# Row-tile loads and transposes in batches of three instead of one by one

## The chip, the cores and the metric

The kernel runs on one core of a Trainium2 chip. The metric is device time in microseconds, the median of several executions. A core has a matrix engine (PE, with its weight loads shown as PEld), a vector engine (DVE), a scalar engine (ACT), GpSimd (POOL) and SyncE (SP). Each works through its own list of instructions in order; semaphores tie the lists together. Here POOL and SP mostly issue DMAs.

## The reference

```python
def reference(x, w1, w2):          # x: 16 x 512 x 1024, w1 and w2: 1024 x 768, float32
    y1 = np.matmul(x, w1)
    y2 = np.matmul(x, w2)
    return (np.tanh(y1) * y2).astype(np.float32)
```

The rows of x are 16 x 512 = 8192, which makes 64 row tiles of 128 rows. Both products have the same left side.

## The kernel before, in words

**Tiles.** A row tile mt (0 to 63) goes through these steps. A load on POOL's queue (`load_x`, L353) brings it from device memory and casts it to fp16 into one of 8 buffers `xh`. A DMA transpose issued by SP (`transpose`, L378) turns it into one of 12 buffers `xT`, so that the contraction lies along the partitions. ACT sums its absolute values (`abs_x`, L381) for a range check at the end.

**Head and triples.** The first 4 tiles (HEAD) are multiplied plainly (`mm`, L421) while the weights come in. The other 60 form 20 triples (i = 0 to 19). Tile HEAD + 3i + r is row r of triple i. Tiles 0 to 6 are transposed by PE; from tile 7 on (BY_PE, so from triple 1) they are transposed by DMA, which makes 57 of them.

**A triple.** Its two halves of K times three row tiles against blocks of the two weights are computed by a scheme with fewer products: 15 products p0 to p14, each 4 matmuls with 512 columns (`product`, L444). Their left sides are either one half of a transposed tile or a sum or difference of such halves, made by DVE (`x_sum`, L412, ten per triple, named S3, S11, ... and written to a part of `early_x`). Their right sides are blocks of the weights `wh` or sums of blocks `b` (`w_sum`, L403). The products are combined in PSUM banks by ACT (`c_copy`, L448) and DVE (`c_add`, L454), then tanh on ACT (`c_tanh`, L457) and the multiplication on DVE (`c_mul`, L462) give the output tile `o`, which a store (L418) on SP's queue writes out. In each triple p7 is first and reads the third tile's transposed half directly; the first sums are S3 (first tile alone) and S11 (S3 with the second tile).

**Order.** PE's order of products is written out by hand (`PE_ORDER`). For the other engines a `Planner` simulates all operations with costs, due times and assumed DMA times, and emits them in the order of their planned starts. What it emits is then fixed for each engine. Its assumptions on when DMAs land (`lands`, `latency`, `LANDING`) thus change only the order, and an instruction that stands too early in an engine's list makes that engine wait.

**Holding the loads.** POOL would issue loads as early as buffers allow. A tiny copy on POOL from a transposed tile (`hold_loads`, L481) makes POOL wait until that transpose has landed:

```python
    def hold_loads(e, mt):
        pin(nc.gpsimd.tensor_copy(held, xt(mt)[:, 0, :1]))
```

Before the change, three loads (7, 8, 9) are free, and each later load mt waits for the transpose of tile max(mt - 4, 7). Transposes follow one another in tile order on SP, each after its own load; stores stand between them where the planner put them.

**Buffers.** A load into `xh` waits until the tile that was there before (8 tiles earlier) was transposed and summed by ACT. A transpose into `xT` waits for the last readers of the tile 12 before it, which is four triples.

Of the kernel before, what the change touches and what calls it, by code (L numbers as in the profile page):

```python
# [74 lines left out]
class Planner:  # L75
# [9 lines left out]
    def op(self, name, engines, due, needs, fn, *args, behind=(), issued=(), chains=(), xfer=0.0, latency=None, seeds=False,  # L85
           lands=None, hold=0.0):
        assert name not in self.ops, name
        self.ops[name] = dict(engines=engines, due=due, needs=[n for n in needs if n], behind=[n for n in behind if n], issued=[n for n in issued if n], fn=fn, args=args,
                              chains=chains, xfer=xfer, latency=latency, seeds=seeds, lands=lands, hold=hold)
        for c in chains:  # L90
            self.chains.setdefault(c, {"left": 0, "bank": None, "end": 0.0, "act": 0.0, "dve": 0.0})["left"] += 1
# [135 lines left out]
def kernel(  # L227
# [13 lines left out]
    MT = B * M // P  # L241
    F = 512
    G = N - F
    HEAD = 4
    TRIPLES = (MT - HEAD) // 3
    BY_PE = HEAD + 3
    FP32 = ((0, 0), (1, 0))
    LOW, HIGH = 512.0, 1024.0
    XT_BUFS, XH_BUFS, S_BUFS, O_BUFS, C_BUFS = 12, 8, 2, 9, 2
    WARM = 512, 512, 512, 512, 512, 512, 512  # L250
    FILL = 512, 512, 256
    AHEAD, FREE = 4, 3
    LANDING = {HEAD + 6: 5.8, HEAD + 7: 4.1, HEAD + 8: 3.9}
    S_AHEAD, HALVED = 4.0, 4
    LATER = {mt: 66.0 + 13.0 * mt for mt in range(HEAD - 1)}
    bf16, f16, f32, i32 = mybir.dt.bfloat16, mybir.dt.float16, mybir.dt.float32, mybir.dt.int32
# [39 lines left out]
    def xh_place(mt):  # L296
        return (mt - HEAD) % XH_BUFS

    def xh_before(mt):
        return next((m for m in range(mt - 1, 1, -1) if xh_place(m) == xh_place(mt)), None)  # L300
# [4 lines left out]
    op = plan.op  # L305
# [203 lines left out]
    rows_in = (HEAD + 2, HEAD, HEAD + 1)  # L509
# [3 lines left out]
    lands = dict(zip("x00 a0 x10 a1 x20 a2 x30 a3".split(), (4.31, 4.47, 6.13, 6.53, 7.7, 8.17, 9.05, 9.44)))  # L513
# [7 lines left out]
    for n, what in enumerate(on_sp):  # L521
        before = [f"L{on_sp[n - 1]}"] if n else []
        if what[0] == "x":
            op(f"L{what}", {"sp": 0.05}, 0.1 * n - 100, [], load_first, int(what[1]), int(what[2]), issued=before, lands=lands[what])
        else:
# [4 lines left out]
               behind=[f"c{a}{b}" for a, b in old], lands=lands[what])  # L530
# [3 lines left out]
    for n, mt in enumerate(rows_in):  # L534
        op(f"L{mt}", {"pool": 0.58}, 1 + 0.1 * n, [], load_x, mt, issued=[f"L{rows_in[n - 1]}" if n else f"c{late[-1]}"],
           behind=[f"cx{m}{h}" for m in range(2, HEAD) for h in range(2) if xh_place(m) == xh_place(mt)], lands=lands[f"x{mt}"])

    landed = {}
    for s, k in slices:
        loads = [f"g{k % KH}{t}" for t in range(2)] if s == "g" else [f"{s}{k}"]  # L540
# [30 lines left out]
    xt_readers = {mt: [] for mt in range(MT)}  # L571
# [12 lines left out]
    def reuse_out(mt):  # L584
        return [f"st{mt - O_BUFS}"] if mt >= HEAD + O_BUFS else []
# [16 lines left out]
    for n, s in enumerate("agb"):  # L602
        for mt in range(HEAD):
            if (s, mt) == ("b", HEAD - 1):
                continue
            due, behind = (lambda n: landed[slices["agb".index(s) * KO + n]] + 0.8 + 0.02 * mt), []
            finals(mt, s, due(KO - 1) + (5.0, 3.0, 7.0)["agb".index(s)], plain(mt, s, due, behind))

    mt = HEAD - 1
# [57 lines left out]
    for i in range(TRIPLES):  # L667
# [3 lines left out]
        for v, a, b, how in A_SUMS:  # L671
            op(f"S{v}.{i}", {"dve": 0.335}, None, x_needs(i, a) + x_needs(i, b), x_sum, i, v, a, b, how,
               hold=needed(i, v) - S_AHEAD if i > 1 else 0.0,
               behind=[f"{r}.{i - S_BUFS}" for r in a_readers[v]] if i >= S_BUFS else first_done)
# [3 lines left out]
        for o in C_OPS:  # L678
# [3 lines left out]
            if kind == "p":  # L682
                needs += x_needs(i, o[4]) + w_needs(o[5])
                op(f"{name}.{i}", {"pe": SLOT}, slot_of[i, name], needs, product, i, *o[3:], chains=chains,
                   behind=[f"m{HEAD - 1}y0{KO - 1}"] if (name, i) == ("p3", TRIPLES - 1) else [])
# [3 lines left out]
            if kind in ("seed", "copy", "add"):  # L689
                before = []  # L690
                if o[3][0] == "s":
                    before = [f"{r}.{i - C_BUFS}" for r in readers[o[3]]] if i >= C_BUFS else all_casts
# [5 lines left out]
            r = o[3]  # L698
            mt = HEAD + 3 * i + r
            due = soonest[i, name] + LAST  # L700
            if kind in ("t", "th"):
                lo, n = (0, F) if kind == "t" else (F, G)
                op(f"{name}.{i}", {"act": 0.5 if n == F else 0.285}, due, needs, c_tanh, i, r, o[4], lo, n, o[5],
                   behind=reuse_out(mt) + ([f"{FIRST_READER[name]}.{i}"] if i == TRIPLES - 1 and name in FIRST_READER else []), chains=chains)
# [4 lines left out]
            else:  # L709
                lo, n, at = (0, F, 0) if kind == "m" else (F, G, G)  # L710
                op(f"{name}.{i}", {"dve": 0.6 if n == F else 0.335}, due + 1, needs, c_mul, i, r, o[4], lo, n, at, chains=chains)
                outs[mt].insert(0 if kind == "m" else 1, f"{name}.{i}")
    for mt in range(MT):
# [14 lines left out]
                op(f"st{mt}{a}", {"sp": 0.4, "act": 0.4}, 2e4, part, store, mt, lo, n, xfer=0.4)  # L728
        else:
            op(f"st{mt}", {"sp": 0.05}, slot_of[max(i, 0), "p2"] + 12, outs[mt], store, mt, behind=late, xfer=1.0)  # L730
    for mt in range(BY_PE, MT):
        back = xh_before(mt)
        free = [] if back is None else ([f"PT{back}0", f"PT{back}1"] if back < BY_PE else [f"T{back}"]) + ([f"D{back}"] if back >= HEAD else [])
        before = f"L{mt - 1}" if mt > BY_PE else f"L{rows_in[-1]}"
        if mt >= BY_PE + FREE:
            op(f"H{mt}", {"pool": 0.1}, None, [f"T{max(mt - AHEAD, BY_PE)}"], hold_loads, max(mt - AHEAD, BY_PE), issued=[before])
            before = f"H{mt}"
        op(f"L{mt}", {"pool": 0.58}, None, [], load_x, mt, issued=[before], behind=free, xfer=XX)
        op(f"T{mt}", {"sp": 0.05}, None, [f"L{mt}"], transpose, mt, issued=[f"T{mt - 1}"] if mt > BY_PE else [],
           behind=xt_readers[mt - XT_BUFS] if mt >= XT_BUFS and mt - XT_BUFS != HEAD - 1 else [], xfer=1.2, latency=LANDING.get(mt, 1.0 if mt < HEAD + 6 else 3.0))  # L740
    for mt in range(HEAD, MT):
        i, r = divmod(mt - HEAD, 3)
        soon = START + 6 + 1.1 * r if i == 0 else slot_of[i, "p7"] + (2, 0, -4, -8)[min(i, 4) - 1] + 4.3 * r
# [125 lines left out]
```

## Time and profile before

| | |
|---|---|
| median of 3 runs | 297.87 us (297.68 to 299.07) |
| the profiled execution | 297.88 us |
| its span, first to last instruction | 296.3 us |
| granted clock of PE, mean | 0.997 |
| DVE busy | 257.4 us (87%) |
| ACT busy | 226.3 us (76%) |
| POOL busy | 49.2 us (17%) |
| DMA: loads of x by POOL | 60, of 256 KB in fp16, median 6.8 us from issue to landing |
| DMA: transposes by SP | 57, median 6.9 us |
| DMA: stores by SP, whole tiles | 58, of 384 KB, median 5.3 us |

The span lies inside the profiled execution's time; 1.6 us are around it. Times in the trace count from the start of the span. PE's busy time overlaps itself, since matmuls are pipelined and their ends are modelled, so rates are read from the starts.

### The profile page before, as it was taken

Reading aid. Unit: us, or ns where it says so; the run is one execution under the profiler, and the core shown is the slowest. Engines: PE = TensorE matmul, PEld = TensorE weight load, DVE = VectorE, ACT = ScalarE, POOL = GpSimd, SP = SyncE. Lnnn points to the kernel's source line nnn. Section 1 sums busy time; section 2 is a strip of 40 time slices with the busy share of each in tenths; the row PEclk is TensorE's granted clock in tenths of the full one; section 3 lists DMA queues with packets and bytes.
Section 4 is the critical chain, followed back from the end, with each engine's and each line's share of the span. In section 5 each row is a group of like instructions: output and inputs, shape, how many; then the busy total and the mean of one; then the engine's idle time right before and its main releaser. Section 6 shows DMA issues by size and latency. Waiting matters only on the chain. (4 is left out here: it accounts for less than half of the span.)

```text
span 296.3 us, 4677 instructions
## 1 busy us (share of the span) xinstructions
PE 289.6 (98%) x1374; PEld 131.9 (45%) x1374; DVE 257.4 (87%) x552; ACT 226.3 (76%) x453; POOL 49.2 (17%) x129
## 2 busy tenths in 40 slices
PE   7999999999999999999999999999999999999994
PEld 3344444444444444444444444444444444444442
DVE  1679899989999998888989898898989989898785
ACT  3586899699978979797797988768686776868442
POOL 0063033020213021102110120031012110000000
PEclk9999999999999999999999999999999999999998
DMA  6999999999999999999999999999999999340334
GB/s 215 388 307 204 183 160 149 229 197 237 224 253 271 215 198 252 237 144 253 233 234 162 221 191 218 195 310 223 221 235 232 261 269 298 127 162 25 136 141 164
DMA packets 84715, 63.51 MB, mean 214 GB/s; under 512 B 62800, under 2 KB 66896, under 8 KB 84688
## 3 DMA queue, kind: packets, MB, share of 16 engines
q1 hardware_dynamic: 73888, 44.84, 62.9%
q0 software_dynamic: 9792, 16.78, 37.2%
q10 hardware_dynamic: 1008, 1.57, 1.5%
q8 instruction: 11, 0.18, 0.3%
q14 instruction: 16, 0.13, 0.2%
HBM read 39.85 MB, written 25.17 MB: 219 GB/s over the span
## 5 line engine op out<-in xcount | busy, mean ns | idle before, releaser
L444 PE MATMUL bank<-b,early_x 128*128 128x512 f16 x640 | 148.3, 379 | 0.1
L444 PEld LDWEIGHTS <-early_x 128*128 128x128 f16 x800 | 78.1, 98 | 95.0 <-issue 0.7
L454 DVE TENSOR_TENSOR bank<-bank,arena 128x512 f32<-128x512 f32 x100 | 69.6, 697 | 14.4 <-ACT arena L448 8.8
L448 ACT ACTIVATE arena<-bank 128x512 f32<-128x512 f32 x100 | 59.4, 596 | 28.7 <-PE bank L444 28.5
L462 DVE TENSOR_TENSOR o<-o,bank 128x256 f32<-128x256 f32 (+1 forms) x132 | 64.3, 512 | 6.1 <-ACT o L457 5.4
L381 ACT ACTIVATE junk<-xh 128x1024 f16<-128x1024 f16 x60 | 63.3, 1054 | 0.2
L444 PEld LDWEIGHTS <-xT 128*128 128x128 f16 x400 | 39.0, 98 | 46.6 <-issue 0.3
L444 PE MATMUL bank<-b,xT 128*128 128x512 f16 x240 | 58.3, 379 | 0.0
L457 ACT ACTIVATE o<-bank 128x256 f32<-128x256 f32 (+1 forms) x80 | 34.5, 436 | 16.0 <-DVE bank L454 11.7
L444 PE MATMUL bank<-wh,xT 128*128 128x512 f16 x160 | 41.1, 379 | 0.0
L444 PE MATMUL bank<-wh,early_x 128*128 128x512 f16 x160 | 40.9, 379 | 0.0
L481 POOL CAST held<-xT 128x1 f32<-128x1 f16 x54 | 12.3, 227 | 159.4 <-DMA xT<-xh 159.3
L353 POOL DMA_DIRECT2D xh<-in_x_dram x60 | 31.9, 532 | 17.2 <-issue 7.7
L412 DVE TENSOR_TENSOR early_x<-early_x,xT 128x512 f16<-128x512 f16 x80 | 33.2, 419 | 0.5
L448 ACT ACTIVATE bank<-bank 128x512 f32<-128x512 f32 x40 | 21.5, 574 | 7.3 <-DVE bank L454 6.2
L457 ACT ACTIVATE o<-arena 128x512 f32<-128x512 f32 x40 | 25.1, 628 | 1.2 <-DVE arena L454 1.2
L421 PE MATMUL bank<-wh,xT 128*128 128x512 f16 x72 | 18.5, 379 | 0.5 <-DVE wh L359 0.3
L412 DVE TENSOR_TENSOR early_x<-xT,xT 128x512 f16<-128x512 f16 x40 | 16.8, 419 | 0.0
L412 DVE TENSOR_TENSOR early_x<-xT,early_x 128x512 f16<-128x512 f16 x40 | 16.8, 419 | 0.0
L454 DVE TENSOR_TENSOR bank<-arena,bank 128x512 f32<-128x512 f32 x20 | 13.9, 695 | 2.4 <-ACT o L457 0.9
L454 DVE TENSOR_TENSOR arena<-bank,arena 128x512 f32<-128x512 f32 x20 | 13.7, 683 | 0.2
L454 DVE TENSOR_TENSOR arena<-arena,bank 128x512 f32<-128x512 f32 x20 | 13.6, 681 | 0.0
(47 smaller groups left out, 134.7 us busy)
## 6 DMA issues: line engine op xcount, KB each, us to landing
out_dram<-o SPq DMA_DIRECT2D x58, 384.0 KB, 5.3
xh<-in_x_dram POOLq DMA_DIRECT2D x60, 256.0 KB, 6.8
arena<-in_w_dram SPq DMA_DIRECT2D x12, 256.0 KB, 5.6
early_x<-in_x_dram SPq DMA_DIRECT2D x8, 256.0 KB, 5.0
arena<-in_w_dram ACTq DMA_DIRECT2D x4, 256.0 KB, 5.9
wh<-in_w_dram POOLq DMA_DIRECT2D x8, 128.0 KB, 5.1
out_dram<-o SPq DMA_DIRECT2D x4, 256.0 KB, 6.5
xT<-xh SPq DMA_TRANSPOSE x57, 6.9
```

The costliest lines, as they stand in the source:

```text
L353: pin(nc.gpsimd.dma_start(xh(mt), xf[mt]))
L381: pin(nc.scalar.activation(junk[:, :src.shape[-1]], src, ACT.Abs, scale=scale, accum_out=sums[:, column:column + 1]))
L412: pin(engine[e].tensor_tensor(x_operand(i, v), x_operand(i, a), x_operand(i, b), OP[how]))
L421: pin(nc.tensor.matmul(bank(chain)[:, :rhs.shape[-1]], xt(mt)[:, k, :], rhs, start=first, stop=k == KO - 1, skip_group_check=True))
L444: pin(nc.tensor.matmul(place(i, dst), x_operand(i, a)[:, k, :], w_rhs(b, k), start=begins and k == 0, stop=k == KH - 1, skip_group_check=T ...
L448: pin(nc.scalar.activation(place(i, dst), place(i, src), ACT.Copy, scale=float(sign)))
L454: pin(nc.vector.tensor_tensor(place(i, dst), a, b, ALU.add if signs == (1, 1) else ALU.subtract))
L457: pin(nc.scalar.activation(out_tile(HEAD + 3 * i + r)[:, lo:lo + n], place(i, src)[:, :n], ACT.Tanh, scale=float(sign)))
L462: pin(nc.vector.tensor_tensor(o, o, place(i, src)[:, at:at + n], ALU.mult))
L481: pin(nc.gpsimd.tensor_copy(held, xt(mt)[:, 0, :1]))
```

## The change

Loads of a triple now form one batch. Three loads are still free. From then on, one hold stands before each group of three loads, and it waits for the second transpose of the triple before. Inside a group the loads are issued in the order second, first, third tile; since transposes stay in tile order, the first transpose of a triple has two loads ahead of it. The planner's assumed landing times are changed as well: nine of them are written out as points in time, and the others have one latency.

```diff
-    AHEAD, FREE = 4, 3
-    LANDING = {HEAD + 6: 5.8, HEAD + 7: 4.1, HEAD + 8: 3.9}
+    FREE = 3
+    LANDING = {7: 36.3, 8: 37.2, 9: 38.2, 10: 44.9, 11: 46.1, 12: 47.3, 13: 53.8, 14: 55.0, 15: 56.2}
...
-    for mt in range(BY_PE, MT):
+    loads = list(range(BY_PE, BY_PE + FREE)) + [mt + r for mt in range(BY_PE + FREE, MT, 3) for r in (1, 0, 2)]
+    for n, mt in enumerate(loads):
         back = xh_before(mt)
         free = ...
-        before = f"L{mt - 1}" if mt > BY_PE else f"L{rows_in[-1]}"
-        if mt >= BY_PE + FREE:
-            op(f"H{mt}", {"pool": 0.1}, None, [f"T{max(mt - AHEAD, BY_PE)}"], hold_loads, max(mt - AHEAD, BY_PE), issued=[before])
+        before = f"L{loads[n - 1] if n else rows_in[-1]}"
+        if n >= FREE and n % 3 == 0:
+            held_by = BY_PE + n - 2
+            op(f"H{mt}", {"pool": 0.1}, None, [f"T{held_by}"], hold_loads, held_by, issued=[before])
             before = f"H{mt}"
         op(f"L{mt}", {"pool": 0.58}, None, [], load_x, mt, issued=[before], behind=free, xfer=XX)
+    for mt in range(BY_PE, MT):
         op(f"T{mt}", {"sp": 0.05}, None, [f"L{mt}"], transpose, mt, issued=[f"T{mt - 1}"] if mt > BY_PE else [],
-           behind=..., xfer=1.2, latency=LANDING.get(mt, 1.0 if mt < HEAD + 6 else 3.0))
+           behind=..., xfer=1.2, latency=2.0, lands=LANDING.get(mt))
```

In the operations' names H is a hold, L a load, T a transpose, each with its tile's number.

More of the change, by code (lines that the diff above doesn't have):

```diff
@@ L730 @@
             op(f"st{mt}", {"sp": 0.05}, slot_of[max(i, 0), "p2"] + 12, outs[mt], store, mt, behind=late, xfer=1.0)
-    for mt in range(BY_PE, MT):
+    loads = list(range(BY_PE, BY_PE + FREE)) + [mt + r for mt in range(BY_PE + FREE, MT, 3) for r in (1, 0, 2)]
+    for n, mt in enumerate(loads):
         back = xh_before(mt)
         free = [] if back is None else ([f"PT{back}0", f"PT{back}1"] if back < BY_PE else [f"T{back}"]) + ([f"D{back}"] if back >= HEAD else [])
-        before = f"L{mt - 1}" if mt > BY_PE else f"L{rows_in[-1]}"
-        if mt >= BY_PE + FREE:
-            op(f"H{mt}", {"pool": 0.1}, None, [f"T{max(mt - AHEAD, BY_PE)}"], hold_loads, max(mt - AHEAD, BY_PE), issued=[before])
+        before = f"L{loads[n - 1] if n else rows_in[-1]}"
+        if n >= FREE and n % 3 == 0:
+            held_by = BY_PE + n - 2
+            op(f"H{mt}", {"pool": 0.1}, None, [f"T{held_by}"], hold_loads, held_by, issued=[before])
             before = f"H{mt}"
         op(f"L{mt}", {"pool": 0.58}, None, [], load_x, mt, issued=[before], behind=free, xfer=XX)
+    for mt in range(BY_PE, MT):
         op(f"T{mt}", {"sp": 0.05}, None, [f"L{mt}"], transpose, mt, issued=[f"T{mt - 1}"] if mt > BY_PE else [],
-           behind=xt_readers[mt - XT_BUFS] if mt >= XT_BUFS and mt - XT_BUFS != HEAD - 1 else [], xfer=1.2, latency=LANDING.get(mt, 1.0 if mt < HEAD + 6 else 3.0))
+           behind=xt_readers[mt - XT_BUFS] if mt >= XT_BUFS and mt - XT_BUFS != HEAD - 1 else [], xfer=1.2, latency=2.0, lands=LANDING.get(mt))
     for mt in range(HEAD, MT):
```

## The prediction

> **What bounds the kernel now.** I read the page's first two parts, then the windows, then the timeline of PE for the rate inside them, and last the waits and the views of the tile xT, because the change touches only loads (L353), holds (L481) and transposes (L378).
>
> The head of the page, with its busy shares:
>
> ```profile
> span 296.3 us, 4677 instructions
> PE 289.6 (98%) x1374; PEld 131.9 (45%) x1374; DVE 257.4 (87%) x552; ACT 226.3 (76%) x453; POOL 49.2 (17%) x129
> ```
>
> The windows; columns are stretch, length, then busy time (and instructions) of PE, PEld, DVE, ACT and POOL, granted clock, DMA share, GB/s:
>
> ```profile
> 30.00:36.00 6.00, 5.87 (x37) 2.78 (x35) 5.41 (x12) 5.43 (x11) 0.00 (x0) 1.00 1.12 167
> 36.00:40.00 4.00, 4.00 (x20) 1.82 (x19) 3.72 (x9) 3.54 (x9) 2.77 (x7) 1.00 0.85 156
> 40.00:50.00 10.00, 10.00 (x48) 4.54 (x47) 9.97 (x24) 9.76 (x20) 2.31 (x5) 1.00 1.20 177
> 50.00:60.00 10.00, 10.00 (x48) 4.43 (x46) 9.95 (x26) 7.24 (x15) 1.58 (x6) 1.00 1.10 205
> 120.00:160.00 40.00, 40.00 (x187) 18.20 (x186) 35.85 (x75) 33.57 (x69) 6.34 (x19) 1.00 1.21 213
> 200.00:240.00 40.00, 40.00 (x187) 18.09 (x185) 35.81 (x74) 29.62 (x59) 6.65 (x18) 1.00 1.18 231
> 280.00:297.00 17.00, 12.17 (x64) 6.02 (x62) 10.40 (x20) 5.92 (x13) 0.00 (x0) 0.93 0.36 134
> ```
>
> PE is busy for all of 36 to 280 us at a granted clock of 1.00. A busy PE need not be a PE at its peak, so I check the rate on the timeline of PE, at the product p7, which opens each triple's 15 products (60 matmuls of 512 columns) and reads a transposed tile directly:
>
> ```profile
> 38.85 1.03 PE L444 MATMUL bank<-wh,xT 128*128 128x512 f16 x4
> 51.80 1.03 PE L444 MATMUL bank<-wh,xT 128*128 128x512 f16 x4
> 271.95 1.03 PE L444 MATMUL bank<-wh,xT 128*128 128x512 f16 x4
> ```
>
> From triple 1 (38.85) to triple 2 (51.80) are 12.95 us, or 216 ns a matmul. From triple 1 to triple 19 (271.95) are 233.10 us for 18 triples: 12.95 again, to the hundredth. So no triple between contains a pause, and none is run slower than another. PE's own program sets the end.
>
> The Trainium skill, "Perfetto Trace Analysis", section Identifying the Most-Contended Engine, says that matmul busy time is a poor measure of headroom and that LDWEIGHTS busy time is a good one. On this page that is 45%, which by that rule would leave over half of PE to win. The spacing of 216 ns speaks against room here: "TensorE: Matmul & The Clock Gate" gives 215.7 ns back to back for 512 columns.
>
> Which waits are there for a transposed tile?
>
> ```profile
> POOL held L481 <- DMA xT<-xh: 159.3, 45, 9.8
> ...
> PE bank L331 <- DVE ones L756: 1.3, 1, 1.3
> ...
> PE bank L371 <- DMA early_x<-in_x_dram: 0.3, 1, 0.3
> ...
> DVE early_x L412 <- DMA xT<-xh: 0.6, 1, 0.6
> PEld L444 <- DVE early_x L412: 0.6, 1, 0.6
> ...
> PE bank L421 <- DVE wh L359: 0.3, 1, 0.3
> ```
>
> POOL waits 159.3 us for transposes, but that is its task: it holds loads back, and POOL is 17% busy. Of those who compute, only one DVE instruction waited for a transpose (0.6 us), and one weight load for DVE (0.6 us). PE's own three waits are those of the start.
>
> **The change, part by part.**
>
> *Room for a gain.* All that this change can give back is what PE loses on account of transposes. PE's idle time in 30 to 36 us is 6.00 - 5.87 = 0.13 us; the weight load's wait is 0.6 us, which may or may not be the same pause. So a gain is at most 0.7 us, 0.25% of the profiled execution's 297.88. The start (PE's waits at L331, L371, L421) lies before the first held load, and the last 4 us after PE's last matmul hold no load.
>
> *Holds.* Before, each load from the fourth on has a hold (54); now each batch of three has one (18). That takes 36 copies from POOL:
>
> ```profile
> L481 POOL CAST held<-xT x54: 185/185/475, 36.4 to 241.2; 128x1 f32<-128x1 f16 x54
> L378 SPq DMA_TRANSPOSE xT<-xh x57: 1231/1776/5876, 31.9 to 247.5; - x57
> L412 DVE TENSOR_TENSOR early_x<-xT x20: 415/416/426, 31.3 to 266.5; 128x512 f16<-128x512 f16 x20
> ...
> DMA to landing us min/median/max: 3.2/6.9/12.6
> ```
>
> At a median of 0.185 us these are 6.7 us of an engine that waits 159 us: nothing on the path. What hides it is POOL's idle time.
>
> *The loop of loads and transposes.* Before, load n waits for transpose n - 4, so a load is usually in flight beside transposes. Now a batch's three loads (second, first, third tile) wait until the second transpose of the batch before has landed, and the first transpose waits for the second load issued. Behind the hold on POOL are only loads; behind a waiting transpose on SP are the next transposes and the stores. The price is therefore one closed loop per triple: hold copy, issue of two loads, landing of the second, transpose, landing of the second transpose. It costs PE nothing while it is shorter than 12.95 us or while there is lead left. The rows for its terms, of the early stretch, first loads and then transposes, and POOL's timeline:
>
> ```profile
> L353 POOL DMA_DIRECT2D xh<-in_x_dram x10: 530/530/530, 36.9 to 61.5; - x10
> DMA to landing us min/median/max: 4.1/5.8/7.1
> ```
> ```profile
> DMA to landing us min/median/max: 3.4/5.1/7.5
> ```
> ```profile
> 36.38 0.37 POOL L481 CAST held<-xT 128x1 f32<-128x1 f16 x1 [9.79 <-DMA xT<-xh]
> 36.89 0.53 POOL L353 DMA_DIRECT2D xh<-in_x_dram  x1
> ...
> 40.22 0.53 POOL L353 DMA_DIRECT2D xh<-in_x_dram  x1 [0.93 <-ACT junk L381]
> 48.22 0.47 POOL L481 CAST held<-xT 128x1 f32<-128x1 f16 x1 [7.47 <-DMA xT<-xh]
> ...
> 49.19 0.42 POOL L481 CAST held<-xT 128x1 f32<-128x1 f16 x1
> ...
> 50.09 0.20 POOL L481 CAST held<-xT 128x1 f32<-128x1 f16 x1
> 50.44 0.53 POOL L353 DMA_DIRECT2D xh<-in_x_dram  x1 [0.15 <-issue]
> ...
> 59.95 0.18 POOL L481 CAST held<-xT 128x1 f32<-128x1 f16 x1 [5.61 <-DMA xT<-xh]
> ```
>
> Fixed terms: the hold copy 0.2, the pause before an issue 0.3, two issues at 0.53 each (1.06), the second transpose behind the first 0.9 (48.22, 49.19 and 50.09 are the holds that the three transposes of triple 2 released): 2.5 us together. A load lands in 4.1 to 7.1 us, a transpose in 3.4 to 7.5. Lower end 2.5 + 4.1 + 3.4 = 10.0; medians 2.5 + 5.8 + 5.1 = 13.4; upper end 2.5 + 7.1 + 7.5 = 17.1 us.
>
> Which of these? The medians are of the old mixture, and the mixture seems to be what makes them long. The load at 36.89 landed after at least 4.1 us, at 41.0, so its transpose could start there; it released its hold at 48.22. The last of the four loads in flight, issued at 40.22, landed by 40.22 + 7.1 = 47.3 at the latest: the transpose came about 1 us after that bound, as if it had stood behind all four loads. The trace also has one batch of the new kind, the first three loads (T7 to T9), with no load issued behind them between 26.6 and 36.89. On SP's timeline and DVE's:
>
> ```profile
> 31.89 17.37 SPq L378 DMA_TRANSPOSE xT<-xh  x7
> 49.37 0.51 SPq L418 DMA_DIRECT2D out_dram<-o  x1
> ```
> ```profile
> 36.28 0.43 DVE L412 TENSOR_TENSOR early_x<-xT 128x512 f16<-128x512 f16 x1 [0.63 <-DMA xT<-xh]
> ...
> 37.56 0.42 DVE L412 TENSOR_TENSOR early_x<-early_x,xT 128x512 f16<-128x512 f16 x1
> ...
> 42.30 0.74 DVE L462 TENSOR_TENSOR o<-o,bank 128x256 f32<-128x256 f32 x2
> ...
> 49.16 0.42 DVE L412 TENSOR_TENSOR early_x<-xT 128x512 f16<-128x512 f16 x1
> 49.61 0.42 DVE L412 TENSOR_TENSOR early_x<-early_x,xT 128x512 f16<-128x512 f16 x1
> ```
>
> T7 was issued at 31.89 (that is when its load had landed), DVE got it at 36.28, and read T8 at 37.56 without a wait. From first issue to second landing that is 5.7 us at most, with the 0.9 inside; and since T7 started behind one load and a first transpose now starts behind two, it is rather less. With that row the loop is 1.6 + 4.1 to 5.8 + 5.7 = 11.4 to 13.1. I take 11.5, near the lower end, by the batch T7 to T9. Then the loop gains 1.4 us on PE per triple, and the lead grows until the buffers stop it (12 xT tiles are four triples; 8 xh tiles under three).
>
> The Trainium skill, "DMA: Bandwidth & Descriptors", section Queues, rings and completion order, speaks against this choice: each DMA engine goes round between its queues packet by packet, so that a transpose would go on beside loads and a batch would shorten nothing. By that, the loop stays at the medians, 13.4 us; the trace's 48.22 does not look like sharing, but nothing here shows a steady stretch of batches. That is the first rival below.
>
> *The first batches, where the lead is small.* T8 has landed by 37.56 at the latest. With the loop's 10.0 to 11.5 us the second transpose of triple 2 (T11) lands at 47.6 to 49.1, the first (T10) 0.9 earlier. DVE reads T10 at 49.16 and T11 at 49.61. T12, another 0.9 behind, is read by PE at 51.80. So triple 2 comes in time by 0.5 to 2 us, about as before (DVE's 49.16 follows the hold's 48.22 by 0.9). Triple 3: T14 11.5 us later at 59.1 to 60.6; before, it released its hold at 59.95. The same again, and from there the lead grows as before.
>
> *Steps that move with it.* The planner's new landing times act only through the order that it writes. That order of instructions changes little elsewhere. On DVE, two instructions (S21 of triple 0 and one B27 half) go ahead of triple 1's first sum, into the 0.63 us that DVE idles before 36.28: worth at most that, and in PE's terms part of the 0.7 above. Triple 2's first sums stand two places earlier. On SP the first store (tile 6) goes ahead of T13 instead of behind it, and store 5 ahead of T16. Tile 6's products are done at about 42.30 + 0.7 = 43.0, before T12 can be issued, so that store waits for nothing and costs T13 its 0.51 us of issue; T13's load lands after it. Later stores change places with transposes in both directions; cover: the lead. After 250 us DVE, ACT and PE keep their order, so the end is the old one. PE's order is the old one throughout; only banks differ.
>
> *Sum.* 297.88 (span 296.3 and 1.6 around it), less 0 to 0.7, plus 0: I take less 0.1, **297.8 us**. The profiled execution stands at the median of the runs, 297.87.
>
> **The rivals.**
>
> *1. Slower: the closed loop is longer than a triple of PE.* Place: hold to second transpose, every triple from 2 on. It decides from 12.95 us on; with a lead of 2 us at most when it begins, a loss appears beyond 12.95 + 2/17 = 13.1 us. At 13.4 the loss is 17 x 0.45 - 2 = 5.7 us: 303.6 us. At 15 it is 17 x 2.05 - 2 = 33 us, 331. For it: the medians of load and transpose, and three stores per triple that share the DMA engines. Against it: the batch T7 to T9, and that the old loop, one hold per load, gave 53 further loads between holds at 36.4 and 241.2, 11.6 us for three, with longer waits in it; by the end it was far ahead (the last triple's first transposed tile is read at 266.5, when all transposes had been issued by 247.5). Chance 0.05.
>
> *2. Slower, once: the first batch comes late.* DVE has no slack in 40 to 60 us (9.97 and 9.95 busy of 10). T10 issued at 37.6 + 1.6 + 4.1 = 43.3 and landing the early stretch's worst 7.5 us later comes at 50.8, 1.6 us after DVE wants it, and PE would pay up to that: 299.5. At the whole trace's worst, 12.6, it is 6.7 us: 304.6. It decides when T10 lands after 49.16. Against it: that 7.5 and 12.6 belong to transposes with newer loads beside them. Chance 0.04, half of it over 0.5%.
>
> *3. Faster by more than the pauses found.* Some of the 216 ns would have to be a disturbance of PE by DMA traffic. Against it: after the last hold at 241.2 hardly a load is left, and PE keeps the same 12.95 us there. It would give 296 us. Chance 0.02.
>
> *4. The change does nothing in the large:* loads end up spaced by other waits (xh tiles, xT tiles) as before. The time is the forecast's, 297.8; I count it there.
>
> **How the numbers follow.** Forecast with the fourth case 0.89; rival 1 0.05, rival 2 0.04, rival 3 0.02. A measurement of this kernel can tell about 0.5%, 1.5 us, from no change: faster beyond that 0.02, within 0.91, slower 0.07. The range: low 297.88 - 0.7 = 297.2, less 0.1 for runs below the median (297.68 is the lowest): 297.1. High: the highest run of before is 299.07, and rival 2's small end lies there too: 299.1. What is left out is rivals 1 and 3 and the far half of 2, about 0.1.
>
> **What would show each step.** Right: p7 of triple 19 again at 271.9 or up to 0.3 earlier, PE full in every window from 36 to 280, 18 holds, and transposes in groups of three whose landing is nearer 4 us than the old median of 6.9. The loop is the distance of two holds that waited in the stretch before the buffers are full: 11.5 expected. Wrong: p7 spaced by more than 12.95 us with DVE or PE waiting for xT (rival 1 if in every triple, rival 2 if once near 50 us); or p7 of triple 19 before 271.2.

## The result: 306.7 us, slower by 2.6%

The changed kernel takes 306.69 us in the median of 6 runs (303.58 to 308.34), the kernel before 297.81. The ratio is 1.026 with a 95% interval of 1.021 to 1.031. The forecast was 297.8 with a range to 299.1, so it was wrong in sign and size. Rival 1, the closed loop, had been given 303.6 us and a chance of 0.05.

The profiled execution of the changed kernel is its slowest, 308.34 us, which the ratio leaves out; the terms below are therefore compared with the other kernels by loop lengths and waits, not by that one time. The head of its page:

```profile
span 306.8 us, 4592 instructions
...
PE 291.6 (95%) x1374; PEld 132.5 (43%) x1374; DVE 255.0 (83%) x552; ACT 224.6 (73%) x453; POOL 43.0 (14%) x93
```

Windows after (columns as before). Up to 120 us PE is as full as it was; then stretches with some 1.5 to 1.9 us of idle PE in 20 appear, at full clock:

```profile
80.00:100.00 20.00, 20.00 (x94) 9.04 (x93) 18.36 (x41) 16.49 (x33) 2.09 (x5) 1.00 0.94 177
100.00:120.00 20.00, 20.00 (x93) 8.94 (x92) 17.77 (x39) 15.99 (x36) 4.01 (x8) 1.00 0.99 204
120.00:140.00 20.00, 18.16 (x85) 8.17 (x84) 16.66 (x35) 14.64 (x31) 3.94 (x8) 1.00 0.94 205
140.00:160.00 20.00, 18.09 (x84) 8.08 (x84) 14.71 (x32) 15.53 (x34) 1.78 (x4) 1.00 0.95 203
180.00:200.00 20.00, 18.47 (x86) 8.24 (x85) 15.26 (x33) 15.92 (x34) 1.78 (x4) 1.00 1.03 203
```

The timeline of PE at p7 of triple 1 and of triple 19:

```profile
38.52 1.03 PE L444 MATMUL bank<-wh,xT 128*128 128x512 f16 x4
282.31 1.03 PE L444 MATMUL bank<-wh,xT 128*128 128x512 f16 x4
```

They were at 38.85 and 271.95. The loss between them is 10.7 us, and it is the whole difference of the spans (10.5).

Waits after, and SP's own:

```profile
POOL held L481 <- DMA xT<-xh: 198.2, 18, 12.1
DVE bank L454 <- ACT arena L448: 25.6, 16, 3.6
...
ACT o L457 <- DMA out_dram<-o: 15.5, 8, 3.0
...
PE bank L444 <- ACT bank L448: 9.0, 8, 1.9
...
DVE early_x L412 <- DMA xT<-xh: 2.7, 6, 0.8
```
```profile
SPq L378 <- DMA xh<-in_x_dram: 141.6, 19, 16.3
```

POOL now waits 198.2 us in 18 holds (159.3 before), SP 141.6 us for loads (71.0 before). The line of before:

```profile
SPq L378 <- DMA xh<-in_x_dram: 71.0, 28, 16.0
```

New is the line "ACT o <- DMA out_dram<-o": a tanh waits because the output buffer that it needs has not been stored yet. Transposed tiles are hardly waited for (2.7 us).

**How a late batch reached PE.** One pause, on SP, ACT and PE:

```profile
132.68 2.65 SPq L378 DMA_TRANSPOSE xT<-xh  x2
135.42 0.55 SPq L418 DMA_DIRECT2D out_dram<-o  x1
136.06 1.28 SPq L378 DMA_TRANSPOSE xT<-xh  x1
```
```profile
138.27 1.15 ACT L457 ACTIVATE o<-arena 128x512 f32<-128x512 f32 x2 [2.96 <-DMA out_dram<-o]
139.32 1.06 ACT L448 ACTIVATE bank<-bank 128x512 f32<-128x512 f32 x2
```
```profile
139.95 1.02 PE L444 MATMUL bank<-wh,early_x 128*128 128x512 f16 x4 [1.84 <-ACT bank L448]
```

The store at 135.42 is that of tile 21. Its data were ready at 108.3 (the end of its last multiplication in the trace), but the planner had put it between two transposes of triple 9, and SP stood before those, waiting for their loads, until 132.68. It landed at 138.2. The tanh of tile 30 uses the same buffer and started at 138.27, after 2.96 us of waiting; behind it on ACT stood the copy that prepares a bank (L448, 139.32); PE's product on that bank began at 139.95, after 1.84 us of idle time. The same chain ends most of PE's pauses from here on.

**The loop itself.** POOL's timeline; each hold that waits marks one turn:

```profile
177.74 0.18 POOL L481 CAST held<-xT 128x1 f32<-128x1 f16 x1 [11.32 <-DMA xT<-xh]
...
191.95 0.18 POOL L481 CAST held<-xT 128x1 f32<-128x1 f16 x1 [12.08 <-DMA xT<-xh]
192.49 1.59 POOL L353 DMA_DIRECT2D xh<-in_x_dram  x3 [0.35 <-issue]
...
205.02 0.18 POOL L481 CAST held<-xT 128x1 f32<-128x1 f16 x1 [10.94 <-DMA xT<-xh]
...
219.08 0.31 POOL L481 CAST held<-xT 128x1 f32<-128x1 f16 x1 [11.93 <-DMA xT<-xh]
```

The turns are 14.2, 13.1 and 14.1 us. The first two turns of the kernel took 11.1 and 11.0 (holds at 37.1, 48.3 and 59.2), the 15 after them 13.5 on average (59.2 to 261.2). PE needs 12.95 per triple. Transposes did get short:

```profile
DMA to landing us min/median/max: 3.1/3.3/5.2
DMA to landing us min/median/max: 4.0/6.8/9.3
```

Transposes land after a median of 3.3 us instead of 6.9; loads still take 6.8.

**How far PE stands behind the loop.** The product p7 reads the triple's third tile. In triple 8 it starts 0.1 us after that tile has landed, but from triple 11 to triple 19 always 6.9 to 7.0 us after it. So PE follows the loop at a fixed distance there, with transposed tiles in hand, and what stops it is the stores that stand behind the transposes. From triple 1 to 19 the third tiles land over 237.1 us, against PE's 233.1: of the 10.7 us lost, 4.0 are the loop's length and 6.7 are this distance.

### The profile page after: what moved, and what is told of

It is laid out like the page before. It is cut to its first block, busy times and chain, and to the rows that moved or that the text cites. A ratio compares the mean times of both kernels' runs of the same rounds, so it can differ in the third digit from the quotient of the medians.

```text
span 306.8 us, 4592 instructions
## 1 busy us (share of the span) xinstructions
PE 291.6 (95%) x1374; PEld 132.5 (43%) x1374; DVE 255.0 (83%) x552; ACT 224.6 (73%) x453; POOL 43.0 (14%) x93
## 5 line engine op out<-in xcount | busy, mean ns | idle before, releaser
L444 PEld LDWEIGHTS <-early_x 128*128 128x128 f16 x800 | 78.1, 98 | 105.6 <-issue 12.7
L448 ACT ACTIVATE arena<-bank 128x512 f32<-128x512 f32 x100 | 59.1, 596 | 19.5 <-PE bank L444 18.8
L457 ACT ACTIVATE o<-bank 128x256 f32<-128x256 f32 (+1 forms) x80 | 33.4, 437 | 15.4 <-DVE bank L454 13.5
L481 POOL CAST held<-xT 128x1 f32<-128x1 f16 x18 | 5.8, 322 | 198.2 <-DMA xT<-xh 198.2
L448 ACT ACTIVATE bank<-bank 128x512 f32<-128x512 f32 x40 | 21.3, 566 | 3.0 <-DVE bank L454 2.2
L381 ACT ACTIVATE junk<-wh 128x768 f16<-128x768 f16 x16 | 13.5, 845 | 0.2
```

What stands on the lines that cost most here:

```text
L381: pin(nc.scalar.activation(junk[:, :src.shape[-1]], src, ACT.Abs, scale=scale, accum_out=sums[:, column:column + 1]))
L444: pin(nc.tensor.matmul(place(i, dst), x_operand(i, a)[:, k, :], w_rhs(b, k), start=begins and k == 0, stop=k == KH - 1, skip_group_check=T ...
L448: pin(nc.scalar.activation(place(i, dst), place(i, src), ACT.Copy, scale=float(sign)))
L457: pin(nc.scalar.activation(out_tile(HEAD + 3 * i + r)[:, lo:lo + n], place(i, src)[:, :n], ACT.Tanh, scale=float(sign)))
```

## The experiments

All are edits of the changed kernel unless said otherwise. Each was compared with the kernel before on the same chip. Rival explanations were that the loop is too long (and then which part of it), that the stores' places on SP's list are the cause, and that the planner's new landing times spoil the order.

**plan_only: the new landing times alone**

```diff
+ # in words: loads in the order (0, 1, 2)
+ if n >= FREE:  held_by = max(mt - 4, BY_PE)        # a hold for each load, as before
- LANDING = {..., 13: 53.8, 14: 55.0, 15: 56.2}
+ LANDING = {...}                                    # 7 to 12 kept
```

> The changed kernel with the old holds (each load after the third waits for the transpose four tiles back) and the old load order, and only the planner's new landing times kept (the three latest written-out ones left to the planner). Loop theory: the closed loop of hold, three loads and transposes is what costs, 13.4 to 14.2 us per triple against PE's 12.95, so without it the time is that of before, 297.8 us. Store theory (stores placed behind late transposes on SP run the o buffers out): no late batch, so 297.8 too. Planner theory (the new landing times give DVE and ACT a worse order): about 306.

Measured 299.23 us, ratio 1.004 (1.002 to 1.006). In its trace, of a run of 298.45 us, most of the loss lies early (triple 1 to 2 in 13.32 us instead of 12.95); where the median's other 0.8 us go, no trace shows. So the landing times cost a little, not 2.6%.

**batch_old_plan: the counterpart, batches with the old landing times**

```diff
- LANDING = {7: 36.3, ...};  latency=2.0, lands=LANDING.get(mt)
+ LANDING = {HEAD + 6: 5.8, HEAD + 7: 4.1, HEAD + 8: 3.9};  latency=LANDING.get(mt, 1.0 if mt < HEAD + 6 else 3.0)
```

> The changed kernel with the planner's old assumptions on landing times; the batches, their holds and the load order are kept. It is the counterpart of the run with the new landing times alone (299.2 us, 1.004 of before). Closed-loop theory: the loop is what costs, 303 to 309 us. Planner theory: near before, 298 to 300.

302.1 us, ratio 1.013 (1.009 to 1.018), a little under the range. The batches alone cost about half; the other half needs the new landing times on top, which by themselves cost 0.4%.

**plan_true: the planner told times near the measured ones**

```diff
- LANDING = {..., 10: 44.9, 11: 46.1, 12: 47.3, 13: 53.8, 14: 55.0, 15: 56.2}
+ LANDING = {..., 10: 46.1, 11: 48.1, 12: 49.3, 13: 57.6, 14: 59.1, 15: 60.4}
- latency=2.0
+ latency=4.5
```

> The changed kernel, same holds and load order, but the planner is told landing times near those measured (tiles 10 to 15 as in the trace of after, later ones with 4.5 us after their data instead of 2.0), so that its batches come every 12.95 us and it puts the stores of third tiles ahead of the transposes that they now wait behind. Loop theory: the loop is as long as before the correction, 304 to 307 us. Store theory: the o buffers come free in time and PE loses at most 1 to 2 us: 298 to 300. Planner theory: better orders on DVE and ACT, 298 to 300, but without any wait of ACT for stores in either.

305.34 us, ratio 1.025 (1.022 to 1.029). Its waits:

```profile
ACT junk L381 <- DMA xh<-in_x_dram: 26.6, 14, 4.1
...
DVE early_x L412 <- DMA xT<-xh: 7.7, 16, 1.2
```

No tanh waits for a store any more: the stores now stand ahead. Instead ACT's sums wait for loads (26.6 us) and DVE for transposes (7.7 us), and the time is the same. The turns of the loop are 13.2 us on average (holds from 37.8 to 262.4 in 17 turns), as in after. Here PE does use up its lead: from triple 13 on, p7 starts 0.6 to 1.2 us after its third tile has landed, but the third tiles land over 239.2 us instead of 237.1. So moving the stores ahead gains nothing while the loop is too long; they were the first to be hit.

**hold_first and hold_third: one transpose fewer, one more in the loop**

```diff
- held_by = BY_PE + n - 2
+ held_by = BY_PE + n - 3      # hold_first
+ held_by = BY_PE + n - 1      # hold_third
```

> The changed kernel with one step of the loop taken out: a batch of loads is held until the first transpose of the batch before, not the second. Loop theory: the loop loses one transpose spacing, 1.3 to 1.9 us, and comes to 11.8 to 12.6 us, under 12.95: PE full again, 297.8 us (297.5 to 299). Store theory: transposes come earlier, so stores do too: 297.8 to 300. Planner theory: the landing times are as in the changed kernel, about 306.

> The changed kernel with one step of the loop added: a batch of loads is held until the third transpose of the batch before. Loop theory: 1.3 to 1.9 us more per triple on a loop that binds already: 15 loops of about 14.9 us, 28 us over before, so 320 to 330 us. Store theory: the stores move with the transposes only once, 306 to 312. Planner theory: 306.

The loop theory failed in both: hold_first took 314.09 us (ratio 1.052, 1.047 to 1.057), hold_third 307.5 (1.030, 1.025 to 1.035), which lies in the range of the store theory. In hold_first the waits, the transposes, and one pause of PE with the windows around it:

```profile
ACT o L457 <- DMA out_dram<-o: 16.8, 4, 6.7
```
```profile
DMA to landing us min/median/max: 3.1/3.5/11.4
```
```profile
213.36 1.01 PE L444 MATMUL bank<-wh,early_x 128*128 128x512 f16 x2 [5.49 <-ACT bank L448]
```
```profile
200.00:220.00 20.00, 14.51 (x57) 6.03 (x56) 10.77 (x23) 8.80 (x18) 1.78 (x4) 0.83 1.11 188
220.00:240.00 20.00, 20.00 (x94) 9.11 (x93) 18.25 (x38) 13.29 (x26) 1.78 (x4) 1.00 0.95 181
```

The loads are now released while the second and third transposes are still moving. The median transpose is as short as in after (3.5), but three third transposes took 10.1 to 11.4 us with newer loads beside them, and a batch's last load landed 10.6 us after the first issue on average (8.7 in after). Three of the four long waits for stores (16.8 us together) fall into those jams, and a pause of PE of 5.5 us that followed took the granted clock with it: 0.83 in that window. In hold_third the longer hold was paid back: a batch's last load landed 8.0 us after the first issue, and a turn took 13.4 us (13.2 in after). So a turn isn't a sum of independent latencies; loads that are released earlier take longer to land.

**small_stores: the stores' bytes out of the loop**

```diff
+ n = n if mt < HEAD else min(n, 128)       # in store(): 128 columns instead of up to 768
```

> The changed kernel with each store of tiles 4 to 63 cut to 128 of its columns (the rest of the output is left unwritten); loads, holds, transposes and all arithmetic stay. Serial-DMA theory (in the closed loop transposes 3.9 us, then the stores behind them on SP 3.5 us, then loads 5 us move one after the other on full DMA engines): the stores' part falls to about 0.6 us, the loop from 13.5 to about 10.5 to 11, as in the first two loops of after (11.2 and 10.9 us): PE is full, 297 to 298.5 us. Latency theory (the loop is the sum of issue and landing latencies, whatever else the engines move): loop still 13 us or more, 303 to 307.

297.69 us, ratio 0.998 (0.995 to 1.001), as the serial-DMA theory had it. POOL's timeline and the loads:

```profile
92.17 0.18 POOL L482 CAST held<-xT 128x1 f32<-128x1 f16 x1 [8.11 <-DMA xT<-xh]
...
104.56 0.18 POOL L482 CAST held<-xT 128x1 f32<-128x1 f16 x1 [10.26 <-DMA xT<-xh]
...
114.72 0.18 POOL L482 CAST held<-xT 128x1 f32<-128x1 f16 x1 [8.04 <-DMA xT<-xh]
```
```profile
DMA to landing us min/median/max: 3.5/5.6/8.3
```

Turns of 12.4 and 10.2 us; over the batches hold to second transpose is 11.6 us (13.2 in after), a little over the expected 10.5 to 11. The loads' median fell from 6.8 to 5.6. In after, SP issues stores right behind the transposes that release the loads, in the turn that starts at 191.95 five:

```profile
191.23 3.69 SPq L418 DMA_DIRECT2D out_dram<-o  x5
```

The packets of this turn stand in this order: to 195.5 three whole-tile stores, to 201.2 the loads (with two smaller stores of the head's tiles among them), to 205.2 the transposes. On average over 17 turns a batch's first packet of a load starts 3.4 us after the hold in after and 1.9 us in small_stores. The stores' part is what this run took out.

**order012, order021, order210: which load comes when.** The holds are those of after.

```diff
- for r in (1, 0, 2)
+ for r in (0, 1, 2)      # or (0, 2, 1), or (2, 1, 0)
```

> The changed kernel with the loads of a batch in the order first, second, third, so that the first transpose waits for one load and not two; holds as in the changed kernel. Serial-DMA theory: the transposes' data move only when the batch's three loads are through, so the second transpose lands no earlier: loop 13.4 to 14, 304 to 308 us. Latency theory: the first transpose is issued one load (1.2 us) earlier and the loop is 1.2 us shorter, about 12.3: 298 to 300. If transposes and loads in flight together hurt, the first transpose lands after more than the 3.3 us of after, and the time is above after's.

> The changed kernel with the loads of a batch in the order first, third, second: the first transpose waits for one load, the second for all three. Issue theory: the second transpose, which ends the loop, is issued when the last load lands and lands 3.1 to 3.3 us later, as in after (3.0): loop 13 to 13.5, 302 to 307 us. Theory that it matters how many loads the first transpose waits for: as with first, second, third, 297.7.

> The changed kernel with the loads of a batch in the order third, second, first, so that the first transpose waits for all three loads. Issue theory (each transpose takes SP 1.25 us to issue and lands 3.3 us later; with one load ahead these issues pass while the later loads drain, with two ahead the second transpose lands 3.0 us after the last load): the second transpose lands 3.3 + 1.3 = 4.6 us after the last load, the loop grows by about 1.5 us to 14.5 to 15, 318 to 330 us. Theory that the DMA engines' total work sets the loop: as after, 304 to 309.

Means over the 17 held batches after the first, from the starts and landings of the traces (us):

| loads' order | hold to last load landed | first transpose issued, against last load | second transpose landed, against last load | hold to second transpose | time | ratio to before |
|---|---|---|---|---|---|---|
| 0, 1, 2 | 9.1 | -3.1 | +2.7 | 11.9 | 297.73 | 0.999 (0.996 to 1.002) |
| 0, 2, 1 | 9.0 | -3.2 | +3.7 | 12.7 | 301.73 | 1.014 (1.011 to 1.017) |
| 1, 0, 2 (after) | 9.3 | -1.3 | +3.9 | 13.2 | 306.69 | 1.026 (1.021 to 1.031) |
| 2, 1, 0 | 9.3 | +0.1 | +4.8 | 14.2 | 321.71 | 1.078 (1.071 to 1.084) |

The loads take the same time in all four; what differs is how many of the transposes' issues are done when the last load lands. SP's timelines of order012, and of order210 below:

```profile
197.81 4.56 SPq L378 DMA_TRANSPOSE xT<-xh  x3
202.46 1.65 SPq L418 DMA_DIRECT2D out_dram<-o  x3
```
```profile
185.18 4.03 SPq L378 DMA_TRANSPOSE xT<-xh  x3
189.26 1.05 SPq L418 DMA_DIRECT2D out_dram<-o  x2
```

One issue takes SP at least 1.23 us, three take 4.0 when nothing else holds them up (order210: 4.03). With the first load in front, the first issue is over before the last load lands, and the second transpose lands 2.7 us behind it. With two loads ahead it is 3.9, with three 4.8. So the serial-DMA theory fails for order012 (it gave 304 to 308), and the DMA engines' work alone doesn't set the loop; the latency theory (298 to 300, a loop of 12.3) came near. The issue theory named the direction for both other orders and sized order210 (318 to 330 us); order021's loop and time came out just under its range. In order021 1.7 us are lost between p7 of triples 1 and 2. The rest comes late, with the stores: tanh waits 8.1 us for them, and p7 starts 6.9 to 7.2 us after its third tile has landed (triples 14 to 19), though the third tiles of triples 1 to 19 land over 230.1 us, less than PE's 233.1.

**order_only: the kernel before with the load order alone**

```diff
+ # in words: loads 7, 8, 9, then each triple as (1, 0, 2); one hold for each load, four places back
```

> The kernel before with the load order second, first, third alone: each load after the third still has a hold of its own on the transpose four places back, and the planner's old landing times stay. Closed-loop theory: no batch, so nothing closes the loop, 297.6 to 299.5 us. If the load order costs by itself (ACT's sums and xh buffers in another order, the first transpose later): 301 or more.

297.82 us, ratio 0.998 (0.995 to 1.001). Without the batch hold the order costs nothing.

**hold_two_back: the loop opened**

```diff
- held_by = BY_PE + n - 2
+ held_by = max(BY_PE + n - 5, BY_PE)
```

> The changed kernel with the holds opened: a batch of loads waits for the second transpose of the batch before the last one, so that the chain hold, loads, transposes spans two triples (25.9 us of PE) and the DMA engines always have a next load. Closed-loop theory in either form: nothing binds, PE is full, 297.5 to 299.5. Mixture theory (a transpose with newer loads beside it takes 10 to 12 us, as three third transposes did when the hold was one transpose earlier, 314 us): as slow or slower, 305 to 320.

306.43 us, ratio 1.025 (1.013 to 1.037): the time lies in the range of the mixture theory, but not in its way. Its windows:

```profile
50.00:60.00 10.00, 5.34 (x18) 1.77 (x16) 6.31 (x16) 3.50 (x8) 2.21 (x5) 0.76 1.10 171
60.00:70.00 10.00, 10.00 (x43) 4.33 (x42) 7.81 (x17) 6.03 (x14) 1.06 (x2) 0.89 1.13 250
...
120.00:290.00 170.00, 170.00 (x790) 77.05 (x789) 151.00 (x316) 131.71 (x265) 18.21 (x40) 1.00 1.04 209
```
```profile
DMA to landing us min/median/max: 3.2/8.3/14.2
```

From 120 to 290 us PE is full, although transposes take a median of 8.3 us among the loads: long transposes cost nothing once there is lead. The whole loss is early, where six loads were let in at once and the lead is small: in before, p7 starts 0.7 us (triple 1) and 2.0 us (triple 2) after its third tile has landed. The granted clock fell to 0.76 in the window of the two pauses, 4.7 us together, and the two triples lost 7.7 us.

## Why the prediction was wrong, step by step

- **PE's program sets the end, at most 0.7 us to win.** Right. The best kernels run here (order012, small_stores, order_only) all stand at 297.7 to 297.8.
- **Transposes in batches land after nearer 4 us.** Right: 3.3 instead of 6.9. The forecast then treated short transposes as a short loop. The Trainium skill states that each DMA engine goes round between its queues packet by packet ("DMA: Bandwidth & Descriptors", Queues, rings and completion order). The prediction took from it, as a rival, that a batch would shorten nothing and the loop stay at 13.4 us. The loop came to 13.2, but by other terms: the transposes did get short and the loads long. No run here tests the rule itself. In a batch of after the first transpose is issued only 1.3 us before the last load has landed, so loads and transposes are hardly in flight together; where they were, as in the jams of hold_first, a transpose took up to 11.4 us.
- **The loop takes 11.5 us.** This is the step that failed, and in it one term, the second load's landing. The sum was 1.6 us up to and with that load's issue, 4.2 for its landing, near the low end of 4.1 to 5.8, and 5.7 for the transposes. The trace has 1.1, 6.9 and 5.2 on average, together 13.2. (The 1.6 counts one issue of 0.5 twice, since a landing time runs from the start of the issue.) The 4.1 to 5.8 were taken from the early stretch, where few stores were in flight. In the batches SP issues up to three whole-tile stores right behind the transposes that release the loads, and the stores move first. small_stores shows that part: with a sixth of their bytes the second load lands after 5.4 us and the turn is 11.6. The rest, 5.4 against 4.2, lay in the choice of the low end. The prediction had named the stores as something for rival 1 and gave them no price.
- **"Behind two loads it is rather less."** Half right: issue to second landing is shorter (5.2 against 5.8 in order012), but it starts 1.8 us later against the last load, a net loss of 1.2 us. That decides: order012, with the same stores, stays under 12.95. The 1.23 us that SP needs for each issue stood in a quoted row and was not used; the spacing of two transposes was put at 0.9 and is 1.4.
- **"Cover: the lead" for the stores on SP.** Wrong. The list of what is queued behind a waiting transpose was there (the next transposes and the stores), but who waits for a store was not followed. ACT's tanh does, and it was the first to stop.
- **Rival 1.** It was right in its place, hold to second transpose, and in its threshold. That its 303.6 us came near is partly luck. It lets PE lose only when the lead is used up; with the trace's mean turn of 13.18 us it gives 17 x 0.23 - 2 = 1.9 us, about 299.8. It had no term for the stores, which stop PE with transposed tiles in hand. The last turns grow to 14 us, when PE's pauses are already part of the loop; what makes them longer was not tried by itself.
- **Rival 2.** It didn't happen in the changed kernel (T10 landed at 46.1), but in hold_two_back (52.3), for the reason given; in order021 (49.2) it is likely behind the early 1.7 us.

What stays open: why the planner's new times add another 1.3% on top of the batches (302.1 to 306.7). plan_true shows only that putting the stores ahead doesn't bring it back. That the loss of after divides into 4.0 and 6.7 us is read from one trace.

## What to carry to other kernels

A hold that waits for the result of the work it releases closes a loop. Price the whole turn with everything that shares its queues, and compare it with the bottleneck's period: against 12.95 here, turns of 11.9 us were free, 13.2 cost 2.6% and 14.2 cost 7.8%. A mean under the period is not enough: order021, at 12.7, lost 1.4%, to a first batch that came late and to stores that stood behind late transposes on SP's list. So follow also what is queued behind the transfer that waits, and who waits for it. Take a transfer's landing time from a stretch with the same neighbours, and put first the load whose consumer is slow to issue. A long median of a transfer with lead is no defect: 8.3 us transposes kept PE full, and making them 3.3 us gained nothing.

## What the runs showed of the hardware

With loads in flight beside it a transpose took up to 11.4 us from issue to landing (hold_first) or 14.2 (hold_two_back); in order210, where from the second batch on all loads have landed before a batch's first transpose is issued, it took 3.0 us at least, 3.3 in the median and 4.8 at most. A pause of PE of 5.5 us (hold_first) or two of 2.3 and 2.4 us close together (hold_two_back) lowered the granted clock in their windows to 0.83 and 0.76, and one of 3.1 us in hold_first lowered it to 0.91 from 120 to 140 us; the pauses of after, 1.9 us at most, left it at 1.00.
